# A state-space mixer's rotated scan, computed in place in the PSUM accumulators

## The chip, the cores and the metric

The kernel runs on one core of one Trainium2 chip. The metric is the device time of one execution, in microseconds (us).

## The reference

The kernel computes a two-layer encoder trunk over 512 tokens of width 1024, all in float32. The first layer mixes tokens with a diagonal complex state space (64 groups of 16 channels, 64 complex states per group), the second with an attention; each is followed by a gated feed-forward layer with a short convolution. The change lies in the state space:

```python
def s5_mixer(xn, w_in, ...):
    u = (xn @ w_in).astype(f32)
    a_bar = jnp.exp(lam * dt)
    b_bar = ((a_bar - 1.0) / lam)[..., None] * b_mat
    bu = jnp.einsum('tbgh,gph->tbgp', u_t.astype(jnp.complex64), b_bar)
    a_cum, s = lax.associative_scan(binop, (a_elems, bu), axis=0)
    s = s + a_cum * h0[None]
    y = jnp.einsum('tbgp,ghp->tbgh', s, c_mat).real
    g = jax.nn.gelu(y + d_skip * u)
    val, gate = jnp.split(g @ w_glu, 2, axis=-1)
    return val * jax.nn.sigmoid(gate)
```

## The kernel before

The 512 tokens are cut into 64 steps of 8 tokens. Within a step a small triangular matrix gives the output directly, and a state is carried only from step to step. The 1024 channels go through in four blocks, q = 0 to 3, of 16 groups each. For one block the work is this:

- `project` multiplies the normed input with the weight (three passes of split float32 on TensorE), `turn` transposes the result.
- `weights` (L1136, its products at L821 to L823) builds on VectorE (DVE) the matrices that inject a step into the state, six operations of 128 x 512 for each half block. They write their products to scratch tiles `tt1` and `tt2`, two buffers each, all operands in SBUF. `turn_weights` transposes the matrices on TensorE.
- `rotations` builds a table `tab` of cosines and sines, on DVE for q = 0, 1 and on GpSimd (POOL) for q = 2, 3; it has one buffer.
- `inject` (L1226) accumulates a block's injected steps in two PSUM banks, 4 (real parts) and 5 (imaginary parts), `self.pv[q]`, each 128 partitions x 512 (8 pairs of groups x 64 steps). No other work of this stage uses these banks.
- `states` (L1239) turns the two banks by the table (L1253 to L1256), so that the complex recurrence becomes two real ones, and scans them (L1258) with the decay `dec`. `rotate` (L1261) turns the result back (L1268, L1269) and writes the states into the tiles `p_s`, one step later (L1272, four operations of 64 partitions x 504).
- `outs` computes output matrices `w2d` on POOL, copied by DMA into `p_w`; `lags` and `toeplitz` make the triangular matrix, by way of a tile `p_ktt` (DVE L1185).
- `output` (L1275) multiplies with that matrix (L1284) and, at L1287, the states `p_s` with `p_w`; ScalarE (ACT) applies the GELU, and `turn_output` (L1301) transposes into bank 7, the bank that `lags` uses as well.

Sixteen DVE operations make the states of a block:

```python
for o, x, y, op in ((v[0], cs, sn, ALU.add), (v[1], sn, cs, ALU.subtract)):
    t1, t2 = tmp()
    tt(out=t1, in0=pv[0], in1=x, op=ALU.mult)
    tt(out=t2, in0=pv[1], in1=y, op=ALU.mult)
```

Only these four products read PSUM; the two sums, two scans, four products and four last operations read two tensors from SBUF each.

The order of TensorE's work is written out by hand in the list `ORDER` (L750): in it `output` of a block always stands ahead of the next block's `inject`. A number in the list runs that many steps of filler on TensorE: the projections of later blocks, then the first half of the gate's matrix product. The order on DVE, ACT, POOL and the DMA queue SP is made by a scheduler when the kernel is built. Weights arrive by DMA in `t_wraw` (three buffers), ACT rounds them to `t_whi`, and the rest `t_wlo` is subtracted on DVE, in this stage mostly on POOL (L130).

Of the kernel before, what the change touches and what calls it, by code (L numbers as in the profile page):

```python
# [7 lines left out]
F32 = mybir.dt.float32  # L8
# [3 lines left out]
ALU = mybir.AluOpType  # L12
PSUM = bass.MemoryType.PSUM

P = 128
T = 512
# [702 lines left out]
C = T // L  # L719
# [58 lines left out]
def flat(t):  # L778
    n = len(t.shape) - 1
    names = "abcd"[:n]  # L780
    return t.rearrange(f"p {' '.join(names)} -> p ({' '.join(names)})")
# [64 lines left out]
class S5:  # L846
# [286 lines left out]
    def tmp(self, shape):  # L1133
        return lambda: (self.t(shape, F32, "tt1", 2), self.t(shape, F32, "tt2", 2))
# [104 lines left out]
    def states(self, q):  # L1239

        nc = self.nc
        K = [P, 8, C]
        dec = self.t(K, F32, "dec")
        nc.scalar.copy(dec, self.rmag[:, 8 * q : 8 * q + 8].unsqueeze(2).broadcast_to(K))
        nc.gpsimd.memset(dec[:, :, 0:1], 0.0)
        pv = self.pv[q]
        cs, sn = (t.rearrange("p a b c -> p (a b c)") for t in self.tab[q])
        tt = nc.vector.tensor_tensor
        v = [flat(self.t(K, F32, f"v{k}")) for k in range(2)]
        tmp = self.tmp([P, T])  # L1250
        for o, x, y, op in ((v[0], cs, sn, ALU.add), (v[1], sn, cs, ALU.subtract)):
            t1, t2 = tmp()
            tt(out=t1, in0=pv[0], in1=x, op=ALU.mult)  # L1253
            tt(out=t2, in0=pv[1], in1=y, op=ALU.mult)
            a, b = (t1, t2) if op == ALU.add else (t2, t1)
            tt(out=o, in0=a, in1=b, op=op)  # L1256
        for k in range(2):
            nc.vector.tensor_tensor_scan(v[k], flat(dec), v[k], 0.0, ALU.mult, ALU.add)  # L1258
        self.rotate(q, [t.rearrange("p (a b) -> p a b", a=8) for t in v], self.tab[q])

    def rotate(self, q, st, tab):  # L1261
        nc = self.nc
        w = lambda t: t[:, :, 0 : C - 1]
        cs, sn = (w(t.rearrange("p a b c -> p a (b c)")) for t in tab)
        tmp = self.tmp([P, 8, C])
        for k, (x, y, op) in enumerate(((cs, sn, ALU.subtract), (sn, cs, ALU.add))):
            t1, t2 = (w(t) for t in tmp())
            nc.vector.tensor_tensor(out=t1, in0=x, in1=w(st[0]), op=ALU.mult)  # L1268
            nc.vector.tensor_tensor(out=t2, in0=y, in1=w(st[1]), op=ALU.mult)  # L1269
            for g in range(2):  # L1270
                pp = slice(64 * g, 64 * g + 64)
                nc.vector.tensor_tensor(  # L1272
                    out=self.s[q % 2][g][64 * k : 64 * k + 64, :, 1:C], in0=t1[pp], in1=t2[pp], op=op)

    def output(self, q, half):  # L1275

# [242 lines left out]
```

## Time and profile before

| What | us |
|---|---|
| median of 3 runs | 1286.46 (1284.4 to 1286.83) |
| the profiled execution, its own time | 1292.35 |
| its span, first to last instruction | 1290.6 |
| busy in the span: PE, DVE, ACT, POOL | 1227.5, 820.9, 541.8, 159.4 |
| granted TensorE clock, mean of the span | 0.972 of full speed |

The profiled execution is 5.9 us longer than the median, and 1.75 us of its time lies outside the span. Starts are in us from the span's start; PE is TensorE's matmuls, PEld its weight loads. The stage that holds the change lies from about 60 to 210 us.

### The profile page before, as it was taken

The page shows a single profiled execution, that of the slowest core. Times are in us where ns is not written, and L with a number is a line of the kernel's source. Part 1 is how long each engine was busy: PE and PEld are TensorE (multiplying, and loading weights), DVE is VectorE, ACT ScalarE, POOL GpSimd, SP SyncE. Part 2 cuts the span into 40 slices and gives each one's busy share as a digit, 9 for nine tenths or more (in the row PEclk, how much of TensorE's full clock was granted, in tenths as well). Part 3 has the DMA queues.
Part 4 walks back from the last instruction along what each step waited for, and adds up shares of the span by engine and source line. Part 5 has one row for each costly group of instructions (what it writes and reads, how often), then busy time and mean ns, then how long its engine had stood idle before and what let it go on. Part 6 is the DMA issues. An engine that isn't in the chain of part 4 may idle for free. (4 is left out here: it accounts for less than half of the span.)

```text
span 1290.6 us, 17189 instructions
## 1 busy us (share of the span) xinstructions
PE 1227.5 (95%) x6815; PEld 1020.9 (79%) x6815; DVE 820.9 (64%) x1252; ACT 541.8 (42%) x869; POOL 159.4 (12%) x133
## 2 busy tenths in 40 slices
PE   7666779999999999999999999999999999999998
PEld 7566667788888888888899888877688888888887
DVE  8997874587655555333368988987675555553222
ACT  7434433344433333222347666654443343332110
POOL 5848662000000000000000000000300000000000
PEclk9778889999999999999999999999999999999999
DMA  7222232323333333333322212112133333332230
GB/s 191 74 74 65 53 93 74 96 84 98 98 98 98 98 98 94 91 90 100 101 83 65 72 61 66 50 49 60 39 115 96 87 96 98 98 98 98 97 129 35
DMA packets 162379, 111.68 MB, mean 87 GB/s; under 512 B 7452, under 2 KB 151868, under 8 KB 162236
## 3 DMA queue, kind: packets, MB, share of 16 engines
q1 hardware_dynamic: 161724, 109.55, 28.9%
q8 instruction: 53, 0.87, 0.3%
q10 hardware_dynamic: 576, 1.05, 0.2%
q14 instruction: 26, 0.21, 0.1%
HBM read 101.93 MB, written 2.10 MB: 81 GB/s over the span
## 5 line engine op out<-in xcount | busy, mean ns | idle before, releaser
L249 PE MATMUL b<-t_xhi,t_whi 128*128 128x512 f32 x864 | 337.2, 393 | 1.4 <-ACT p_w L1327 1.4
L250 PE MATMUL b<-t_xlo,t_whi 128*128 128x512 f32 x864 | 337.4, 391 | 0.8 <-DVE t_xlo L168 0.7
L251 PE MATMUL b<-t_xhi,t_wlo 128*128 128x512 f32 x864 | 337.5, 391 | 0.2 <-DVE t_wlo L130 0.2
L116 ACT CAST t_whi<-t_wraw 128x1024 fp32r<-128x1024 f32 (+1 forms) x166 | 172.5, 1041 | 357.9 <-PE b L250 243.9
L130 DVE TENSOR_TENSOR t_wlo<-t_wraw,t_whi 128x1024 fp32r<-128x1024 f32 x152 | 184.8, 1217 | 155.7 <-ACT t_whi L116 155.0
L249 PEld LDWEIGHTS b<-t_xhi,t_whi 128*128 128x128 f32 x864 | 162.7, 188 | 37.8 <-issue 2.1
L250 PEld LDWEIGHTS b<-t_xlo,t_whi 128*128 128x128 f32 x864 | 162.6, 188 | 36.6 <-DVE t_xlo L168 2.6
L251 PEld LDWEIGHTS b<-t_xhi,t_wlo 128*128 128x128 f32 x864 | 162.5, 188 | 34.7 <-DVE t_wlo L130 0.6
L457 PE MATMUL b<-t_whi,t_xhi 128*128 128x256 f32 x384 | 109.6, 286 | 0.0
L458 PE MATMUL b<-t_wlo,t_xhi 128*128 128x256 f32 x384 | 109.2, 285 | 0.0
L459 PE MATMUL b<-t_whi,t_xlo 128*128 128x256 f32 x384 | 108.7, 285 | 0.0
L314 DVE TENSOR_TENSOR p_fg<-b,p_rsrow 128x512 f32<-128x512 f32 x44 | 30.4, 690 | 87.0 <-PE b L251 80.6
L325 DVE TENSOR_TENSOR p_fv<-b,p_rsrow 128x512 f32<-128x512 f32 x44 | 30.3, 689 | 69.6 <-PE b L251 69.6
L457 PEld LDWEIGHTS b<-t_whi,t_xhi 128*128 128x128 f32 x384 | 73.3, 191 | 1.6 <-issue 1.2
L459 PEld LDWEIGHTS b<-t_whi,t_xlo 128*128 128x128 f32 x384 | 73.1, 191 | 1.5 <-issue 1.4
L458 PEld LDWEIGHTS b<-t_wlo,t_xhi 128*128 128x128 f32 x384 | 73.4, 191 | 0.3
L249 PE MATMUL b<-p_ahi,t_whi 128*128 128x512 f32 x176 | 69.3, 394 | 0.0
L250 PE MATMUL b<-p_alo,t_whi 128*128 128x512 f32 x176 | 69.3, 394 | 0.0
L251 PE MATMUL b<-p_ahi,t_wlo 128*128 128x512 f32 x176 | 69.3, 394 | 0.0
L348 PE MATMUL b<-t_wlo,p_ahi 128*128 128x512 f32 x176 | 69.3, 394 | 0.0
L347 PE MATMUL b<-t_whi,p_ahi 128*128 128x512 f32 x176 | 69.0, 392 | 0.0
L349 PE MATMUL b<-t_whi,p_alo 128*128 128x512 f32 x176 | 68.3, 388 | 0.0
(304 smaller groups left out, 1989.6 us busy)
## 6 DMA issues: line engine op xcount, KB each, us to landing
t_wraw<-in_ffn_w_up_dram SPq DMA_DIRECT2D x88, 512.0 KB, 3.9
t_wraw<-in_ffn_w_down_dram SPq DMA_DIRECT2D x30, 512.0 KB, 3.4
t_wraw<-in_a_w_glu_dram SPq DMA_DIRECT2D x16, 512.0 KB, 3.6
t_wraw<-in_w_kv_dram SPq DMA_DIRECT2D x16, 512.0 KB, 3.4
t_wraw<-in_ffn_w_down_dram SPq DMA_DIRECT2D x16, 448.0 KB, 3.6
t_wraw<-in_a_w_in_dram SPq DMA_DIRECT2D x8, 512.0 KB, 3.7
p_w<-p_w2d SPq DMA_DIRECT2D x32, 128.0 KB, 2.3
t_wraw<-in_b_w_q_dram SPq DMA_DIRECT2D x8, 512.0 KB, 4.2
```

Source lines behind the costliest of these rows:

```text
L116: nc.scalar.copy(hi, t)
L130: eng.tensor_tensor(out=lo, in0=t, in1=hi, op=ALU.subtract)
L249: nc.tensor.matmul(ps, whi, xhi, start=start, stop=False)
L250: nc.tensor.matmul(ps, whi, xlo, start=False, stop=False)
L251: nc.tensor.matmul(ps, wlo, xhi, start=False, stop=stop)
L314: nc.vector.tensor_tensor(out=g, in0=pg, in1=rr, op=ALU.mult)
L347: nc.tensor.matmul(pss[tb], xh, whi[:, j], start=k + j == 0, stop=False)
L348: nc.tensor.matmul(pss[tb], xh, wlo[:, j], start=False, stop=False)
L349: nc.tensor.matmul(pss[tb], xl, whi[:, j], start=False, stop=st)
L457: nc.tensor.matmul(reg[tb], xh, whi[:, j], start=st, stop=False, skip_group_check=True)
L458: nc.tensor.matmul(reg[tb], xh, wlo[:, j], start=False, stop=False, skip_group_check=True)
L459: nc.tensor.matmul(reg[tb], xl, whi[:, j], start=False, stop=k == 7, skip_group_check=True)
```

## The change

The two banks are rotated, scanned and rotated back where they are. A block's states are still sixteen DVE operations of the same sizes, two of them scans. The scratch tiles `v0` and `v1` are gone, only the two products with the sine go to `tt1` and `tt2`, each time they are needed, and every one of the sixteen has one operand in PSUM and one in SBUF; eight of them write PSUM (four products with the cosine, two sums, two scans), the others SBUF. On the way back the products take all 64 steps instead of 63. `rotate` is merged into `states`, and the lines behind move up by seven.

```diff
--- before.py
+++ after.py
@@ -1243,34 +1243,27 @@
         dec = self.t(K, F32, "dec")
         nc.scalar.copy(dec, self.rmag[:, 8 * q : 8 * q + 8].unsqueeze(2).broadcast_to(K))
         nc.gpsimd.memset(dec[:, :, 0:1], 0.0)
-        pv = self.pv[q]
+        pv = [t[:, :] for t in self.pv[q]]
         cs, sn = (t.rearrange("p a b c -> p (a b c)") for t in self.tab[q])
         tt = nc.vector.tensor_tensor
-        v = [flat(self.t(K, F32, f"v{k}")) for k in range(2)]
-        tmp = self.tmp([P, T])
-        for o, x, y, op in ((v[0], cs, sn, ALU.add), (v[1], sn, cs, ALU.subtract)):
-            t1, t2 = tmp()
-            tt(out=t1, in0=pv[0], in1=x, op=ALU.mult)
-            tt(out=t2, in0=pv[1], in1=y, op=ALU.mult)
-            a, b = (t1, t2) if op == ALU.add else (t2, t1)
-            tt(out=o, in0=a, in1=b, op=op)
-        for k in range(2):
-            nc.vector.tensor_tensor_scan(v[k], flat(dec), v[k], 0.0, ALU.mult, ALU.add)
-        self.rotate(q, [t.rearrange("p (a b) -> p a b", a=8) for t in v], self.tab[q])
-
-    def rotate(self, q, st, tab):
-        nc = self.nc
-        w = lambda t: t[:, :, 0 : C - 1]
-        cs, sn = (w(t.rearrange("p a b c -> p a (b c)")) for t in tab)
-        tmp = self.tmp([P, 8, C])
-        for k, (x, y, op) in enumerate(((cs, sn, ALU.subtract), (sn, cs, ALU.add))):
-            t1, t2 = (w(t) for t in tmp())
-            nc.vector.tensor_tensor(out=t1, in0=x, in1=w(st[0]), op=ALU.mult)
-            nc.vector.tensor_tensor(out=t2, in0=y, in1=w(st[1]), op=ALU.mult)
+
+        t1, t2 = self.tmp([P, T])()
+        tt(out=t1, in0=pv[1], in1=sn, op=ALU.mult)
+        tt(out=t2, in0=pv[0], in1=sn, op=ALU.mult)
+        for k, (t, op) in enumerate(((t1, ALU.add), (t2, ALU.subtract))):
+            tt(out=pv[k], in0=pv[k], in1=cs, op=ALU.mult)
+            tt(out=pv[k], in0=pv[k], in1=t, op=op)
+            nc.vector.tensor_tensor_scan(pv[k], flat(dec), pv[k], 0.0, ALU.mult, ALU.add)
+
+        w = lambda t: t.rearrange("p (a b) -> p a b", a=8)[:, :, 0 : C - 1]
+        t1, t2 = self.tmp([P, T])()
+        tt(out=t1, in0=pv[1], in1=sn, op=ALU.mult)
+        tt(out=t2, in0=pv[0], in1=sn, op=ALU.mult)
+        for k, (t, op) in enumerate(((t1, ALU.subtract), (t2, ALU.add))):
+            tt(out=pv[k], in0=pv[k], in1=cs, op=ALU.mult)
             for g in range(2):
                 pp = slice(64 * g, 64 * g + 64)
-                nc.vector.tensor_tensor(
-                    out=self.s[q % 2][g][64 * k : 64 * k + 64, :, 1:C], in0=t1[pp], in1=t2[pp], op=op)
+                tt(out=self.s[q % 2][g][64 * k : 64 * k + 64, :, 1:C], in0=w(pv[k])[pp], in1=w(t)[pp], op=op)
 
     def output(self, q, half):
```

The scheduler moves some instructions, since scratch buffers come free at other times.

DVE, the second half of the states of block 0 (`b_4_850` and `b_5_851` are the two banks, `p_tt_…` the scratch). Before:

```order
L1258 SCALAR_TENSOR_TENSOR p_v_899<-p_dec,p_v_899 128x512
L1258 SCALAR_TENSOR_TENSOR p_v_900<-p_dec,p_v_900 128x512
L1268 TENSOR_TENSOR p_tt_913<-p_tab_868,p_v_899 128x8x63
L1268 TENSOR_TENSOR p_tt_919<-p_tab_869,p_v_899 128x8x63
L1269 TENSOR_TENSOR p_tt_914<-p_tab_869,p_v_900 128x8x63
L1269 TENSOR_TENSOR p_tt_920<-p_tab_868,p_v_900 128x8x63
L1272 TENSOR_TENSOR p_s_144<-p_tt_913,p_tt_914 64x8x63
L1272 TENSOR_TENSOR p_s_145<-p_tt_913,p_tt_914 64x8x63
L1272 TENSOR_TENSOR p_s_144<-p_tt_919,p_tt_920 64x8x63
L1272 TENSOR_TENSOR p_s_145<-p_tt_919,p_tt_920 64x8x63
```

Now:

```order
L1256 SCALAR_TENSOR_TENSOR b_4_850<-p_dec,b_4_850 128x512
L1256 SCALAR_TENSOR_TENSOR b_5_851<-p_dec,b_5_851 128x512
L1261 TENSOR_TENSOR p_tt_910<-b_4_850,p_tab_869 128x512
L1263 TENSOR_TENSOR b_4_850<-b_4_850,p_tab_868 128x512
L822 TENSOR_TENSOR p_tt_1088<-p_gim,p_b_430 128x512
L1260 TENSOR_TENSOR p_tt_909<-b_5_851,p_tab_869 128x512
L1263 TENSOR_TENSOR b_5_851<-b_5_851,p_tab_868 128x512
L821 TENSOR_TENSOR p_tt_1087<-p_gre,p_b_429 128x512
L1266 TENSOR_TENSOR p_s_144<-b_4_850,p_tt_909 64x8x63
L1266 TENSOR_TENSOR p_s_145<-b_4_850,p_tt_909 64x8x63
L1266 TENSOR_TENSOR p_s_144<-b_5_851,p_tt_910 64x8x63
L1266 TENSOR_TENSOR p_s_145<-b_5_851,p_tt_910 64x8x63
```

Two products of the next block's weights (L822, L821), which had stood behind the states, now stand within them, ahead of the operations that write `p_s`. The same holds for blocks 1 and 2; in block 3 nothing is drawn in.

DVE, from the last `p_s` of block 2 to the `p_ktt` behind it. Before:

```order
L1272 TENSOR_TENSOR p_s_144<-p_tt_1836,p_tt_1837 64x8x63
L1272 TENSOR_TENSOR p_s_145<-p_tt_1836,p_tt_1837 64x8x63
L821 TENSOR_TENSOR p_tt_1885<-p_gre,p_b_429 128x512
L822 TENSOR_TENSOR p_tt_1886<-p_gim,p_b_430 128x512
L821 TENSOR_TENSOR p_tt_1890<-p_gre,p_b_430 128x512
L822 TENSOR_TENSOR p_tt_1891<-p_gim,p_b_429 128x512
L823 TENSOR_TENSOR p_w_1883<-p_tt_1885,p_tt_1886 128x512
L823 TENSOR_TENSOR p_w_1884<-p_tt_1890,p_tt_1891 128x512
L1185 SCALAR_TENSOR_TENSOR p_ktt<-p_eye,p_gain,b_7_1941 128x16
```

Now:

```order
L1266 TENSOR_TENSOR p_s_145<-b_5_1666,p_tt_1815 64x8x63
L823 TENSOR_TENSOR p_w_1865<-p_tt_1867,p_tt_1868 128x512
L821 TENSOR_TENSOR p_tt_1872<-p_gre,p_b_430 128x512
L822 TENSOR_TENSOR p_tt_1873<-p_gim,p_b_429 128x512
L823 TENSOR_TENSOR p_w_1866<-p_tt_1872,p_tt_1873 128x512
L1185 SCALAR_TENSOR_TENSOR p_ktt<-p_eye,p_gain,b_7_1923 128x16
```

Four operations of the weights stand between them where there were six.

POOL, the rotation table of block 2 (`p_tab`) and the splits of streamed weights (`t_wlo`) around it. Before:

```order
L130 TENSOR_TENSOR t_wlo<-t_wraw,t_whi 128x1024
L821 TENSOR_TENSOR p_tp_1789<-p_e16c 128x512
L822 TENSOR_TENSOR p_tp_1790<-p_e16s 128x512
L1245 MEMSET p_dec 128x8
L130 TENSOR_TENSOR t_wlo<-t_wraw,t_whi 128x1024
L823 TENSOR_TENSOR p_tab_1787<-p_tp_1789,p_tp_1790 128x512
```

Now:

```order
L821 TENSOR_TENSOR p_tp_1777<-p_e16c 128x512
L822 TENSOR_TENSOR p_tp_1778<-p_e16s 128x512
L130 TENSOR_TENSOR t_wlo<-t_wraw,t_whi 128x1024
L1245 MEMSET p_dec 128x8
L823 TENSOR_TENSOR p_tab_1775<-p_tp_1777,p_tp_1778 128x512
L130 TENSOR_TENSOR t_wlo<-t_wraw,t_whi 128x1024
```

The splits have moved behind two products and behind the first half of the table. SP issues two of the streamed weight loads one place earlier, ahead of copies of `p_w` and `p_tz`. TensorE and ACT keep their order.

## Rows read from the trace of the kernel before

**Rows 1.** The page's busy time of TensorE: us, share of the span, instructions.

```profile
PE 1227.5 (95%) x6815; PEld 1020.9 (79%) x6815; DVE 820.9 (64%) x1252; ACT 541.8 (42%) x869; POOL 159.4 (12%) x133
```

**Rows 2.** Windows: stretch, us, busy us (instructions) PE PEld DVE ACT POOL, PEclk, DMA, GB/s.

```profile
90.00:95.00 5.00, 4.02 (x29) 3.30 (x29) 4.94 (x8) 0.05 (x1) 1.06 (x1) 0.50 0.00 0
...
127.00:132.00 5.00, 4.22 (x36) 3.53 (x34) 4.97 (x4) 0.52 (x1) 4.84 (x4) 0.54 0.00 0
...
150.00:156.00 6.00, 6.00 (x77) 5.04 (x79) 1.01 (x3) 2.35 (x7) 5.41 (x5) 0.50 0.03 8
...
230.00:1290.00 1060.00, 1053.96 (x5329) 871.01 (x5327) 637.12 (x997) 437.10 (x658) 23.96 (x24) 1.00 0.29 86
```

**Rows 3.** Waits of PE, 60 to 230 us: waiter, releaser, us in total, times, longest.

```profile
PE b L1287 <- DVE p_s L1272: 21.9, 8, 8.3
PE b L1301 <- DVE p_ktt L1185: 11.0, 2, 6.0
```

**Rows 4.** Timeline of DVE, the states of block 0: start us, us, line, tiles.

```profile
70.87 1.29 DVE L1253 TENSOR_TENSOR p_tt<-b,p_tab 128x512 f32<-128x512 f32 x2 [1.21 <-PE b L1235]
...
74.47 4.49 DVE L1258 TENSOR_TENSOR_SCAN p_v<-p_dec,p_v 128x512 f32<-128x512 f32 x2
...
85.37 6.24 DVE L1272 TENSOR_TENSOR p_s<-p_tt,p_tt 64x504 f32<-64x504 f32 x4
```

**Rows 5.** Timeline of DVE, the states of blocks 1 to 3 and the `p_ktt` behind.

```profile
108.51 1.28 DVE L1253 TENSOR_TENSOR p_tt<-b,p_tab 128x512 f32<-128x512 f32 x2
...
122.82 5.26 DVE L1272 TENSOR_TENSOR p_s<-p_tt,p_tt 64x504 f32<-64x504 f32 x4
...
149.70 0.22 DVE L1185 SCALAR_TENSOR_TENSOR p_ktt<-p_eye,p_gain,b 128x16 f32<-128x16 f32 x1
...
156.57 1.29 DVE L1253 TENSOR_TENSOR p_tt<-b,p_tab 128x512 f32<-128x512 f32 x2 [1.15 <-POOL p_tp L821]
...
160.18 1.22 DVE L1258 TENSOR_TENSOR_SCAN p_v<-p_dec,p_v 128x512 f32<-128x512 f32 x1
...
164.92 6.59 DVE L1272 TENSOR_TENSOR p_s<-p_tt,p_tt 64x504 f32<-64x504 f32 x4
...
180.74 0.22 DVE L1185 SCALAR_TENSOR_TENSOR p_ktt<-p_eye,p_gain,b 128x16 f32<-128x16 f32 x1
...
188.24 1.29 DVE L1253 TENSOR_TENSOR p_tt<-b,p_tab 128x512 f32<-128x512 f32 x2 [4.77 <-PE b L1235]
...
200.50 4.91 DVE L1272 TENSOR_TENSOR p_s<-p_tt,p_tt 64x504 f32<-64x504 f32 x4
```

**Rows 6.** DVE's L1272: its group (us, mean ns), then its durations, min/median/max.

```profile
L1272 DVE TENSOR_TENSOR p_s<-p_tt,p_tt 64x504 f32<-64x504 f32 x16 | 22.7, 1419 | 0.3
...
L1272 DVE TENSOR_TENSOR p_s<-p_tt,p_tt x16: 665/1454/2817, 85.4 to 202.6; 64x504 f32<-64x504 f32 x16
```

**Rows 7.** Timeline of POOL: one shape, beside SBUF-only DVE work, then beside L1253.

```profile
84.87 1.54 POOL L1210 TENSOR_TENSOR p_tp<-p_pwim,p_c 128x512 f32<-128x512 f32 x1
...
108.39 1.11 POOL L1210 TENSOR_TENSOR p_tp<-p_pwim,p_c 128x512 f32<-128x512 f32 x1
```

**Rows 8.** Timeline of PE, matmuls that waited: start us, us, line, tiles, [idle before].

```profile
90.16 0.69 PE L1287 MATMUL b<-p_w,p_s 128*64 128x128 f32 x2 [8.26 <-DVE p_s L1272]
...
126.67 0.69 PE L1287 MATMUL b<-p_w,p_s 128*64 128x128 f32 x2 [7.45 <-DVE p_s L1272]
...
149.97 1.11 PE L1301 MATMUL b<-t_ident,p_gl 64*128 64x64 f32 x8 [4.92 <-DVE p_ktt L1185]
...
169.90 0.43 PE L1287 MATMUL b<-p_w,p_s 128*64 128x128 f32 x2 [0.29 <-DVE p_s L1272]
...
171.56 0.32 PE L1287 MATMUL b<-p_w,p_s 128*64 128x128 f32 x1 [1.23 <-DVE p_s L1272]
...
181.01 1.11 PE L1301 MATMUL b<-t_ident,p_gl 64*128 64x64 f32 x8 [6.05 <-DVE p_ktt L1185]
...
205.46 0.32 PE L1287 MATMUL b<-p_w,p_s 128*64 128x128 f32 x1 [2.42 <-DVE p_s L1272]
```

## The prediction

> **What bounds the kernel now.** First the page: TensorE is busy for 1227.5 of 1290.6 us [rows 1], so only the time in which it stands still or runs slowly can be won. The windows show that from 230 us on it is busy for 1053.96 of 1060 us at full clock [rows 2]: whatever shift the first 210 us gain or lose reaches the end unchanged. The waits of PE between 60 and 210 us name two releasers, both on DVE: `p_s`, the states, 21.9 us in eight waits, and `p_ktt`, 11.0 us in two [rows 3]. Together 33 us. `p_ktt` is a tiny operation, late only because DVE works through its queue in order, behind the states and the weights.
>
> Next, what DVE does in the states. In block 0 six operations take from 70.87 to 74.47, so 0.60 us each [rows 4]. The two scans behind them take 4.49, that is 2.25 each, and the four last operations 6.24, that is 1.56 each. In block 2 a scan takes 1.22 [rows 5], and of the last operations the quickest takes 0.665 and the mean 1.419 [rows 6]. So the same operation has two prices. What sets them is POOL: one shape of its takes 1.54 beside an SBUF-only operation of DVE and 1.11 beside the two L1253 at 108.51 [rows 7], which themselves take their usual 1.28 for two [rows 5]. Two SBUF operands on DVE and work on POOL slow each other; with one operand in PSUM neither is slowed. The states pay this in twelve of sixteen operations.
>
> **The change, part by part.** The count of operations is unchanged, so nothing is saved but this overlap; every one of the sixteen now has one PSUM operand.
>
> *Price of a block.* Fourteen operations at 0.60 make 8.4. The two scans have 1.22 as the price without POOL, less the 0.08 by which neighbours overlap (two L1253 take 1.28, 0.60 and 0.68): 2.3. Together 10.7 us. Nothing in the trace writes PSUM from DVE, and no scan reads it. Below, nothing is left to gain beyond 0.60 and 1.14; above, the ends are 1.56 for an operation and 2.25 for a scan, which POOL's overlap costs now. I take the low prices, since the nearest row, an operation of the same size that reads PSUM, has them with POOL at work. A scan that stays at 2.25 would add 2.2 us a block.
>
> *What is drawn in.* In blocks 0 to 2 two products of the weights now stand ahead of `p_s`. They are SBUF-only: 0.60 to 1.56 each. In blocks 0 and 1 POOL is at work, so I take 1.56, 3.1 for two; in block 2 POOL is idle for most of the time, so 1.2. Blocks 0 and 1 then take 13.8, block 2 11.9. Block 3 draws nothing in, but has, as before, two small operations of others within it, 0.8: 11.5. Now they take 20.7, 19.6, 14.9 and 17.2 (70.87 to 91.61, 108.51 to 128.08, 156.57 to 171.51, 188.24 to 205.41) [rows 4, 5].
>
> *What of it reaches TensorE,* in order, each step starting from the shift of the one before:
>
> 1. Block 0 ends at 70.87 + 13.8 = 84.7 instead of 91.6: 6.9 us. TensorE got to its wait at 90.16 - 8.26 = 81.9 [rows 8], so it still waits and takes over all of the 6.9.
> 2. From there to the states of block 1 the chain runs over TensorE and ACT and moves as a whole. Start 101.6, end 115.4 instead of 128.1: shift 12.7. TensorE gets there at 119.2 - 6.9 = 112.3, so it waits again.
> 3. From 128.08 to the `p_ktt` at 149.70 DVE does nineteen operations, 1.14 each with the overlap as it is. Two of them were drawn in; seventeen take 19.3, so 134.7: shift 15.0. TensorE would be there at 145.05 - 12.7 = 132.3 and waits 2.4.
> 4. Block 2 starts at 141.6 and ends at 153.5. TensorE gets there at 169.61 - 15.0 = 154.6. Both waits, 0.29 and 1.23 [rows 8], are gone: shift 16.5.
> 5. To the `p_ktt` at 180.74 six operations take 9.2 now, 1.54 each. Four remain, 6.2: 159.7, a shift of 21.0. TensorE is there at 174.96 - 16.5 = 158.5.
> 6. Block 3 starts at 167.2 and ends at 178.7; TensorE wants the last of it at 203.0 - 21.0 = 182.0, and its wait of 2.42 is gone: shift 23.4.
>
> *What is moved elsewhere.* On POOL the weight splits stand one to two products later, 1.1 to 1.5 each [rows 7]; no wait of TensorE on a split stands beside the long ones of the stage [rows 3], and POOL's own products get shorter. I cost it at nothing; uncovered it would be some 3 us once. The loads that SP issues earlier pass copies of `p_w` and `p_tz` whose readers TensorE starts only after the states: nothing, as long as the buffer for the load is free. The banks are held until the last `p_s`, but TensorE's hand-written order has `output` of the block, which waits for that, ahead of the next `inject`: no new wait.
>
> The sum is -23.4. The profiled execution would come to 1292.35 - 23.4 = 1269.0. It lies 5.9 us above the median of the runs shown; from the median, 1286.46 - 23.4 = **1263 us**.
>
> [...] The rows give 0.60 us for an operation with a PSUM operand and for one without [rows 4], so PSUM itself costs nothing here. [...]
>
> **The rivals.**
>
> *A. The overlap comes back on the weights.* POOL's work is the same; what no longer meets the states may meet the weights' products. For it: the last six, with POOL at work, already take 1.54 each. Against it: POOL's own operations get shorter, so it is done sooner. If step 3's sixteen products all take 1.56, that is 25.6 with the split, `p_ktt` comes at 141.0 and the shift there is 8.7. Block 2 with 13.8 then ends at 161.7, shift 9.8 at its `p_s` and, with four products at 1.56, 12.8 at the next `p_ktt`. With the last 2.4 that is 15: 1271 us.
>
> [...]
>
> *C. Writing PSUM is dear.* Eight operations a block write to PSUM from DVE, two of them scans, and read the same bank. If each took 1.2 us more (three times 0.60 for a plain one), a block would take 9.6 more: 23.4, 23.4, 21.5 and 21.1. Block 0 is then 2.7 late, block 1 another 3.8; the two drawn-in products give back 2.3 in front of `p_ktt`; block 2 loses 6.6 and gets 3.1 back, block 3 loses 3.9. That is 11.6 slower: 1298 us. It turns from a gain to a loss at about 0.8 us more for each. Against it is only that reading costs nothing.
>
> *D. Nothing changes.* TensorE could be held at the same points by something else than the states, a `p_w` copy or a split. No such releaser stands beside the two [rows 3].
>
> **How the numbers follow.** The forecast, 1257 to 1269, has a chance of 0.55; A 0.20, B 0.15, C 0.06, D 0.04. The range leaves out C and D and half of what A and B could overshoot. Its upper end is A with both scans of blocks 0 and 1 at 2.25 (4.4 us): 1275. Its lower end is B with the drawn-in products of blocks 0 and 1 at 0.60 (1.9 us): 1253. A measurement of this kernel can tell about 0.2%, 2.6 us. Forecast, A and B are all faster by more than that; C is slower and D within: 0.90, 0.04 and 0.06.
>
> **What would show it.** The products, sums and last operations of the states at 0.60 to 0.68 us, the scans at about 1.2, with POOL at work beside them; a block's states in 11 to 14 us from first to last; TensorE's total wait for `p_s` below 8 us and for `p_ktt` below 6; POOL's operations beside the states at 1.1. The forecast is wrong if a PSUM-writing operation takes clearly more than 0.7, if the weights' products behind the states go to 1.56 throughout (A), or if a new releaser, a split or a `p_w` copy, stands ahead of TensorE's waits.

## The result and the profile after

| What | before | after |
|---|---|---|
| median of 4 runs, us | 1286.3 (1284.4 to 1286.83) | 1267.6 (1265.56 to 1269.87) |
| the profiled execution, us | 1292.35 | 1265.56 |
| its span, us | 1290.6 | 1263.8 |
| granted TensorE clock, mean of the span | 0.972 | 0.983 |

The ratio is 0.9858, with an interval of 0.9838 to 0.9877: faster by 18.7 us, where 23.4 were forecast. The two profiled executions lie 26.8 us apart; why more than the medians is told with the steps. The page's busy line after, to set against [rows 1]:

```profile
PE 1221.5 (97%) x6815; PEld 1016.3 (80%) x6815; DVE 802.1 (63%) x1252; ACT 542.3 (43%) x869; POOL 152.8 (12%) x133
```

The counts are the same. DVE is 18.8 us less busy and POOL 6.6, with not one instruction fewer: operations on both engines have become shorter. By line, from 60 to 215 us (DVE; busy us, mean ns, then idle before):

```profile
L822 DVE TENSOR_TENSOR p_tt<-p_gim,p_b 128x512 f32<-128x512 f32 x12 | 18.7, 1562 | 0.0
...
L1266 DVE TENSOR_TENSOR p_s<-b,p_tt 64x504 f32<-64x504 f32 x16 | 10.8, 678 | 0.3
L1256 DVE TENSOR_TENSOR_SCAN b<-p_dec,b 128x512 f32<-128x512 f32 x8 | 9.5, 1214 | 0.0
L1254 DVE TENSOR_TENSOR b<-b,p_tab 128x512 f32<-128x512 f32 x8 | 5.5, 690 | 0.0
```

L1266 is L1272 of before: 678 ns where it was 1419 [rows 6]. The scans (L1256) take 1.21 us each throughout, and an operation that reads and writes its own bank (L1254) takes 0.69. The weights' products, all SBUF, are now the long ones: L822 has a mean of 1.56. The waits of PE from 60 to 230 us, against [rows 3] (L1280 was L1287, L1294 was L1301):

```profile
PE b L1280 <- DVE p_s L1266: 6.0, 5, 2.3
PE b L1192 <- DVE p_ktt L1185: 5.3, 2, 4.2
PE b L1179 <- DVE t_xlo L165: 4.6, 1, 4.6
...
PE b L1294 <- DVE p_ktt L1185: 1.4, 2, 1.1
```

The wait for `p_s` has gone from 21.9 to 6.0 and that of L1294 for `p_ktt` from 11.0 to 1.4. The second row, another `p_ktt`, was there before with 5.3. The third is new in this size: a split of activations, `t_xlo`, in DVE's queue behind the weights' products. DVE's timeline after, which answers to [rows 4, 5]:

```profile
71.26 0.69 DVE L1252 TENSOR_TENSOR p_tt<-b,p_tab 128x512 f32<-128x512 f32 x1 [1.61 <-PE b L1235]
...
74.86 2.33 DVE L1256 TENSOR_TENSOR_SCAN b<-p_dec,b 128x512 f32<-128x512 f32 x2
...
78.28 1.46 DVE L822 TENSOR_TENSOR p_tt<-p_gim,p_b 128x512 f32<-128x512 f32 x1
...
80.86 1.68 DVE L821 TENSOR_TENSOR p_tt<-p_gre,p_b 128x512 f32<-128x512 f32 x1
82.45 2.79 DVE L1266 TENSOR_TENSOR p_s<-b,p_tt 64x504 f32<-64x504 f32 x4
...
111.76 2.79 DVE L1266 TENSOR_TENSOR p_s<-b,p_tt 64x504 f32<-64x504 f32 x4
114.58 1.24 DVE L823 TENSOR_TENSOR p_w<-p_tt,p_tt 128x512 f32<-128x512 f32 x1
...
117.21 1.55 DVE L822 TENSOR_TENSOR p_tt<-p_gim,p_b 128x512 f32<-128x512 f32 x1
...
137.21 0.22 DVE L1185 SCALAR_TENSOR_TENSOR p_ktt<-p_eye,p_gain,b 128x16 f32<-128x16 f32 x1
...
141.46 0.69 DVE L1252 TENSOR_TENSOR p_tt<-b,p_tab 128x512 f32<-128x512 f32 x1 [0.32 <-issue]
...
148.61 2.44 DVE L822 TENSOR_TENSOR p_tt<-p_gim,p_b 128x512 f32<-128x512 f32 x1
...
152.78 2.79 DVE L1266 TENSOR_TENSOR p_s<-b,p_tt 64x504 f32<-64x504 f32 x4
...
161.43 0.23 DVE L1185 SCALAR_TENSOR_TENSOR p_ktt<-p_eye,p_gain,b 128x16 f32<-128x16 f32 x1
...
166.62 0.69 DVE L1252 TENSOR_TENSOR p_tt<-b,p_tab 128x512 f32<-128x512 f32 x1 [2.86 <-PE b L1235]
...
175.59 2.79 DVE L1266 TENSOR_TENSOR p_s<-b,p_tt 64x504 f32<-64x504 f32 x4
```

Two scans took 4.49 in block 0 and now 2.33; four last operations took 6.24, 5.26, 6.59 and 4.91, and now 2.79 in every block. Within the blocks only operations of others that were drawn in are still slowed beside POOL: 1.46, 1.68 and 2.44 us (78.28, 80.86, 148.61), and one of 1.32 at 108.72. The two others take 0.68 (111.16, 152.18). POOL's side after, against [rows 7]:

```profile
102.48 1.12 POOL L1210 TENSOR_TENSOR p_tp<-p_pwim,p_c 128x512 f32<-128x512 f32 x1
...
121.38 1.55 POOL L1210 TENSOR_TENSOR p_tp<-p_pwim,p_c 128x512 f32<-128x512 f32 x1
...
148.10 2.41 POOL L130 TENSOR_TENSOR t_wlo<-t_wraw,t_whi 128x1024 fp32r<-128x1024 f32 x1 [3.86 <-ACT t_whi L116]
```

Beside the states of block 1 the shape takes 1.12, beside the weights' products at 121 us 1.55. The `t_wlo` at 148.10 is what makes the drawn-in L822 at 148.61 take 2.44. Windows after, columns as in [rows 2] (the third number from the end is the granted clock):

```profile
90.00:95.00 5.00, 5.00 (x62) 4.62 (x60) 5.00 (x6) 3.56 (x7) 3.26 (x3) 1.00 0.49 108
...
118.00:124.00 6.00, 6.00 (x50) 5.64 (x49) 6.00 (x6) 1.57 (x3) 4.77 (x4) 0.65 0.60 139
...
136.00:142.00 6.00, 5.71 (x105) 4.57 (x104) 2.98 (x6) 4.75 (x12) 5.79 (x4) 1.00 0.03 10
...
180.00:186.00 6.00, 6.00 (x63) 4.94 (x64) 0.00 (x0) 3.59 (x6) 2.38 (x1) 1.00 0.49 145
```

Behind the wait for the states of block 0 the clock is 1.00 where it was 0.50 [rows 2]; behind that of block 1 it is still low for a while (0.65); behind `p_ktt` it is 1.00.

### The profile page after: what moved, and what is told of

The parts are those of the page before. It is cut to its first block, busy times and chain, and to the rows that moved or that the text cites. A ratio compares the mean times of both kernels' runs of the same rounds, so it can differ in the third digit from the quotient of the medians.

```text
span 1263.8 us, 17184 instructions
## 1 busy us (share of the span) xinstructions
PE 1221.5 (97%) x6815; PEld 1016.3 (80%) x6815; DVE 802.1 (63%) x1252; ACT 542.3 (43%) x869; POOL 152.8 (12%) x133
```

## The experiments

All ratios are to the kernel before, run beside it on the same chip.

**1. The kernel before, again.**

> The kernel before, unchanged. The profiled execution that the prediction was made from took 1292.35 us, 6 us more than the median. If that was the one execution's chance, the shifts that its rows give are sound and only the median's distance is off: this run's profiled execution takes 1284 to 1288 and one of its stretches is about 6 us shorter, outside the states. If profiling adds 6 us to this kernel, it takes 1290 to 1294 again. The states of block 0 take 20 to 21 us, of blocks 1 to 3 19 to 20, 14 to 16 and 16 to 18 either way.

Edit: none. Measured 1285.4 us (ratio 1.0001, 0.9981 to 1.0021). Of its ten executions seven lie between 1284.99 and 1285.63, three between 1291.86 and 1292.93; 21 others of the same kernel, timed beside it, fill the gap from 1284.81 up to 1292.47. So the profiled execution of before, 1292.35, stands at the long end and the one profiled here, 1285.16, at the short end: profiling does not add the 6 us. Of the blocks' lengths expected here two were missed: the states of blocks 0 to 3 take 20.8, 20.1, 18.6 and 14.4, so they change from one execution to the next. PE's timeline here:

```profile
147.11 0.70 PE L1301 MATMUL b<-t_ident,p_gl 64*128 64x64 f32 x8 [2.41 <-DVE p_ktt L1185]
...
209.93 0.71 PE L1301 MATMUL b<-t_ident,p_gl 64*128 64x64 f32 x8
```

The wait for the first `p_ktt` is 2.41 instead of 4.92 [rows 8]: the operations between the states of block 1 and that `p_ktt` take 19.5 us instead of 21.6, presumably because they happen to meet POOL less. The eight transposes behind it take 0.70 instead of 1.11, and the granted clock is 1.00 in 147 to 153 where it was 0.50 in 150 to 156. From that `p_ktt` to the states of block 2 it takes 4.24 us instead of 6.87. At the start of block 2 this execution is 5.5 us ahead, and by L1301's last group 7.24 (209.93 against 217.17), the whole difference of the two.

**2. The changed kernel, twice again.**

> The changed kernel, unchanged, on the same chip. Ratio 0.984 to 0.988. States of block 0 in 14.0 us, blocks 1 and 2 in 12.9 to 14.1, block 3 in 11.8.

> The changed kernel again, beside the one before it, for their difference on one chip: 1264 to 1270.

Edit: none. 1268.63 us (ratio 0.9857, 0.9832 to 0.9882), and with the last experiment 1267.12 (0.983, 0.9806 to 0.9854). In the profile of the first, `p_ktt` behind block 1 comes at 138.05, and block 0 takes 14.1 us. TensorE's rows there, then two windows:

```profile
133.59 1.08 PE L1179 MATMUL b<-p_w,p_cm 128*32 128x128 f32 x16 [6.43 <-DVE t_xlo L165]
...
139.99 0.71 PE L1294 MATMUL b<-t_ident,p_gl 64*128 64x64 f32 x8
```

```profile
130.00:136.00 6.00, 2.41 (x23) 1.99 (x24) 5.97 (x6) 1.47 (x6) 5.84 (x5) 0.50 0.20 44
136.00:142.00 6.00, 6.00 (x67) 5.11 (x69) 2.27 (x4) 4.22 (x8) 2.26 (x2) 0.71 0.02 4
```

The wait for `t_xlo` is 6.4, the longest single one; the granted clock in 130 to 136 is 0.50 (0.72 in the first profile), and 0.71 in the next 6 us (1.00). TensorE comes to the transposes at 139.99, when `p_ktt` is long there, and from `p_ktt` to the states of block 2 it takes 5.9 us, where the first profile of the change has 4.25. The other repeat shows the same: 6.4 for `t_xlo`, clock 0.50 and 0.77 in these windows, 5.9 us. So of three profiles of the change one has the short stretch.

**3. The same order, with the states in SBUF.**

> The order of the operations as in the changed kernel (two sine products to scratch, everything else in place), but in place in two SBUF tiles; only the first four products read PSUM. Theory, overlap with POOL: twelve operations have two SBUF operands again, so the states take 17 to 22 us in blocks 0 and 1 (with three products of the weights drawn in), and the time is that of the kernel before within 5 us: 1281 to 1291. Rival, the saving comes from the fewer scratch tiles and from the new order on DVE: 1265 to 1272.

```diff
+        v = [flat(self.t(K, F32, f"v{k}")) for k in range(2)]
...
-            tt(out=pv[k], in0=pv[k], in1=cs, op=ALU.mult)
-            tt(out=pv[k], in0=pv[k], in1=t, op=op)
-            nc.vector.tensor_tensor_scan(pv[k], flat(dec), pv[k], 0.0, ALU.mult, ALU.add)
+            tt(out=v[k], in0=pv[k], in1=cs, op=ALU.mult)
+            tt(out=v[k], in0=v[k], in1=t, op=op)
+            nc.vector.tensor_tensor_scan(v[k], flat(dec), v[k], 0.0, ALU.mult, ALU.add)
+        pv = v
```

1285.22 us (0.9975, 0.996 to 0.999): nearly all of the gain is gone. DVE by line, from 60 to 215 us:

```profile
L1268 DVE TENSOR_TENSOR p_s<-p_v,p_tt 64x504 f32<-64x504 f32 x16 | 21.1, 1321 | 0.3
...
L1257 DVE TENSOR_TENSOR_SCAN p_v<-p_dec,p_v 128x512 f32<-128x512 f32 x8 | 14.7, 1857 | 0.0
```

The mean of a last operation is back at 1.32 and of a scan at 1.86; PE's wait for `p_s` is 27.3. So it is not the new order of the sixteen operations that pays, but the operand in PSUM. Three products of the weights are drawn in here, and blocks 0 and 1 take 22.9 and 20.6 us. The two scratch tiles are back too; that it is not their absence that pays shows in experiment 6, whose second half has them and still gains 13.8.

**4. The states unbroken.** The states and the weights keep the order of the program on DVE, so that nothing is drawn into a block's states.

> The changed kernel, with the operations of the states and of the weights held in program order on DVE, so that no product of the weights stands within the states, and the small operations behind the states of block 1 come ahead of the weights that are not needed yet. Theory, DVE's queue in front of p_s and p_ktt is what TensorE still waits for: states of blocks 0 and 1 in 11 us, waits for p_s under 3 us in total, p_ktt behind block 1 some 5 us earlier, 1257 to 1264. Rival, the products have to be done anyway and only change places: 1265 to 1270.

```diff
-        tt = nc.vector.tensor_tensor
+        tt = lambda **k: self.e.tc.keep_in_program_order(nc.vector.tensor_tensor(**k))
...
-        cmul(self.nc.vector, self.tmp(W), w1[0], w1[1], gb, bb)
+        cmul(Kept(self.e), self.tmp(W), w1[0], w1[1], gb, bb)
```

(`Kept` does for the weights what the first lambda does; the scans are kept likewise, and the four products stand ahead of the two sums.) 1277.42 us (0.9938, 0.9914 to 0.9962), some 9 us slower than the change, outside both expectations; its runs spread from 1273.45 to 1282.70, and the profile is of the shortest. The states do shorten as both said: block 0 takes 11.0 us (69.25 to 80.26), as the prediction priced it. But the wait for `p_s`, expected below 3, is 8.4, and PE's waits from 60 to 230 us show a new one:

```profile
PE b L1163 <- DVE p_w L851: 10.7, 2, 7.1
PE b L1291 <- DVE p_s L1256: 8.4, 7, 3.6
PE b L1305 <- DVE p_ktt L1193: 6.2, 1, 6.2
```

What was put off is the weights, and TensorE needs those as well. DVE's timeline here shows the rest:

```profile
122.89 1.78 DVE L851 TENSOR_TENSOR p_tt<-p_gre,p_b 128x512 f32<-128x512 f32 x1
...
141.69 0.21 DVE L1193 SCALAR_TENSOR_TENSOR p_ktt<-p_eye,p_gain,b 128x16 f32<-128x16 f32 x1
...
144.84 0.23 DVE L1464 COPY t_vc<-b 128x66 f32<-128x66 f32 x1 [2.94 <-PE b L1463]
```

Twelve operations of the weights stand between 122.89 and 140.91, nine of them at 1.44 to 1.78, ahead of the `p_ktt` that comes at 141.69, later than in the change and not earlier as expected; and a small copy, `t_vc`, that waits for TensorE now stands ahead of the states of block 2. They start at 144.99 (141.46 in the change). The two drawn-in products cost a block's states 2 to 3 us, but putting them off lost more, as the sum shows. How the 9 us divide between the weights, `t_vc` and the other order of products and sums was not taken apart.

**5. Before and after with a quieter POOL.**

> The kernel before, with the 48 products and sums that POOL makes for the output matrices left out (ACT copies the coefficients instead, two copies for each half block, so the outputs are not the reference's). POOL keeps the weight splits and the tables of blocks 2 and 3. Theory, overlap with POOL: the SBUF-only operations of the states fall towards 0.6 to 0.7 us, scans to 1.2 where no split or table runs; blocks 0, 1 and 3 in 11 to 16 us; 1262 to 1278. Rival, the SBUF-only operations are slow by themselves or by their order: blocks 0 and 1 in 19 to 21 us, 1280 to 1290.

> The changed kernel with the same work of POOL left out. Theory, overlap with POOL: the change now gains only what splits and tables cost, 2 to 9 us against the quiet kernel before (18.7 with POOL at work), and the weights' products behind the states fall to 0.6 to 0.8 us as well: 1254 to 1264. Rival: the same gain of 15 to 20 us between the two quiet kernels.

```diff
-        mul(tp[0], ar, cr)
-        mul(tp[1], ai, cn)
-        nc.gpsimd.tensor_tensor(out=w2d[0], in0=tp[0], in1=tp[1], op=ALU.add)
...
+        for k in range(2):
+            nc.scalar.copy(w2d[k], self.c[k][:, sl].unsqueeze(2).broadcast_to(W))
```

Before: 1258.31 us (0.978, 0.9766 to 0.9795), faster than either theory expected; after: 1249.03 (0.971, 0.9696 to 0.9725), faster than expected too. The difference between the two forms is 9.3 us instead of 18.7, just above the 2 to 9 expected. Where POOL is idle, the form of before has the low prices too: its last operations of block 0 take 2.78 for four, while those of block 1 stand beside what POOL still does:

```profile
75.31 2.78 DVE L1263 TENSOR_TENSOR p_s<-p_tt,p_tt 64x504 f32<-64x504 f32 x4
...
105.73 5.26 DVE L1263 TENSOR_TENSOR p_s<-p_tt,p_tt 64x504 f32<-64x504 f32 x4
```

So the partner of the overlap is POOL. The weights' products stay near 1.0 in the mean, where 0.6 to 0.8 was expected, as the tables and splits still meet them (1.55 each at 105 to 110 us), and both kernels have a new wait of TensorE of some 5 us for `p_u`, an operation of ACT, which now makes the copies. The tables and the splits stayed on POOL, so the remaining 9.3 us are not a bound on a gain without it; taking those away as well was not tried.

**6. Each half of the change alone.** First the way in (products, sums) in PSUM, with a scan that writes SBUF and the way back in SBUF; then the way in in SBUF, with a scan that writes the bank and the way back in PSUM.

> The changed kernel, in place in PSUM only up to the scans, which write SBUF tiles; the rotation back has two SBUF operands again. Theory, overlap with POOL: the scans of blocks 0 and 1 go from 2.25 to 1.14, the sums to 0.60, some 5 us in all four blocks, and three products of the weights drawn in ahead of p_s take part of it back: 1279 to 1287. Rival, the scan is what matters: 1268 to 1274.

```diff
-            nc.vector.tensor_tensor_scan(pv[k], flat(dec), pv[k], 0.0, ALU.mult, ALU.add)
+            nc.vector.tensor_tensor_scan(v[k], flat(dec), pv[k], 0.0, ALU.mult, ALU.add)
+        pv = v
```

> The changed kernel, with the first rotation in SBUF tiles; the scan reads SBUF and writes the PSUM banks, and the rotation back is in place there. Theory, overlap with POOL: most of the gain is in the eight operations behind the scan (23 of 29 us of DVE time in the rows of before); scans with two SBUF operands stay near 2.25 beside POOL: 1269 to 1276. Rival, the scan is what matters: 1280 to 1287.

```diff
-            tt(out=pv[k], in0=pv[k], in1=cs, op=ALU.mult)
-            tt(out=pv[k], in0=pv[k], in1=t, op=op)
-            nc.vector.tensor_tensor_scan(pv[k], flat(dec), pv[k], 0.0, ALU.mult, ALU.add)
+            tt(out=v[k], in0=pv[k], in1=cs, op=ALU.mult)
+            tt(out=v[k], in0=v[k], in1=t, op=op)
+            nc.vector.tensor_tensor_scan(pv[k], flat(dec), v[k], 0.0, ALU.mult, ALU.add)
```

The way in alone: 1278.26 us (0.9937, 0.9922 to 0.9952), 8.0 faster than before, a little more than expected. The way back alone: 1272.45 (0.9893, 0.9876 to 0.9909), 13.8 faster. Together 21.8, a little more than the 18.7 of both; presumably they shorten the same waits, which was not followed up. By line on DVE, from 60 to 215 us, the way in alone:

```profile
L1268 DVE TENSOR_TENSOR p_s<-p_v,p_tt 64x504 f32<-64x504 f32 x16 | 21.2, 1327 | 0.3
...
L1257 DVE TENSOR_TENSOR_SCAN p_v<-p_dec,b 128x512 f32<-128x512 f32 x8 | 9.5, 1204 | 0.0
```

The same view of the way back alone:

```profile
L1257 DVE TENSOR_TENSOR_SCAN b<-p_dec,p_v 128x512 f32<-128x512 f32 x8 | 11.7, 1484 | 0.0
L1267 DVE TENSOR_TENSOR p_s<-b,p_tt 64x504 f32<-64x504 f32 x16 | 10.8, 678 | 0.3
```

An operation that reads a bank has the low price throughout (by line, means of 678 to 690 ns, and 1204 for a scan); one that reads SBUF only has it where POOL leaves it alone (2.78 for four in experiment 5). The scan shows it best: reading a bank and writing SBUF it takes 1.20; reading SBUF and writing a bank it takes 1.48 in the mean, 2.34 for the two of block 0 and 4.49, the full price of the overlap, for the two of block 1.

**7. One of the weights' scratch products in a bank.** The two banks are free until a block's inject, so from the second half of block 1 on the first product of a pair goes there, and the sum reads it there.

> The changed kernel, with one of the two scratch products of the weights written to the PSUM banks 4 and 5, from the second half of block 1 on, while the banks wait for the next block; the ten sums L823 then have one PSUM operand. The products still read two SBUF tensors. Theory, the weights in front of p_ktt are slowed by POOL: the sums fall from 1.5 to 0.6 us, the p_ktt behind block 1 comes 3 to 5 us earlier, 1259 to 1265. Rival, POOL's operations only meet the products instead, or a bank is now waited for by inject: 1266 to 1272, with a new wait of TensorE's L1235 on DVE in the second case.

```diff
-        cmul(self.nc.vector, self.tmp(W), w1[0], w1[1], gb, bb)
+        tmp = self.tmp(W)
+        if (q, half) > (1, 0):
+            ps = iter((4, 5))
+            tmp = lambda: (
+                self.e.bank(next(ps)).rearrange("p (a l h) -> p a l h", a=4, l=L), self.t(W, F32, "tt2", 2))
+        cmul(self.nc.vector, tmp, w1[0], w1[1], gb, bb)
```

1263.54 us in five runs (1261.72 to 1264.87; 0.9805, 0.9781 to 0.9829), beside 1267.12 (1266.71 to 1267.78) of the change: 3.6 us better, and the fastest version here that leaves no work out. The two ratio intervals overlap, since the kernel before scatters; the runs beside each other don't, though one of experiment 2 (1264.37) lies among them. DVE by line, from 60 to 215 us:

```profile
L821 DVE TENSOR_TENSOR b<-p_gre,p_b 128x512 f32<-128x512 f32 x10 | 13.5, 1368 | 0.1
...
L823 DVE TENSOR_TENSOR p_w<-b,p_tt 128x512 f32<-128x512 f32 x10 | 6.4, 682 | 0.1
```

The sums fall from a mean of 1200 to 682 ns. The products into the bank stay at 1368, since both their inputs lie in SBUF. `p_ktt` comes at 133.52, where the profile of the change taken beside it has 137.36, and the wait for `t_xlo` is 3.3 instead of 6.4. The inject has a new wait of 2.1 for a sum, as the second theory said; that it gives part of the gain back is likely, not shown.

## Why the prediction was right, and where it missed

**The cause** was right. The same sixteen operations in the same order with SBUF operands lose the gain (experiment 3), and each half alone gains where its operations read a bank (experiment 6). The runs add the price of the overlap for an operation with two SBUF inputs: 0.60 to some 1.56 us on DVE, and 1.11 to 1.55 on POOL.

**What would show it** came as said: `p_s` 6.0 (below 8), `p_ktt` at L1294 1.4 (below 6), POOL beside the states at 1.1. **The price of a block** was right. Without anything drawn in, experiment 4 gives 11.0 us for 10.7. The low ends were the right ones: 0.68 to 0.69 for an operation, overlap with its neighbour included, and 2.33 for two scans, with POOL at work.

**The steps**, as time lost (+) or won (-) against the forecast, in the profiled execution:

| Step | predicted | measured | against the forecast |
|---|---|---|---|
| 1. block 0 ends | 84.7 | 85.24 | +0.5 |
| 2. block 1 starts, ends | 101.6, 115.4 | 101.60, 114.55 | -0.5, -0.9 |
| 3. the `p_ktt` | 134.7 | 137.21 | +3.4 |
| 4. block 2 starts, ends | 141.6, 153.5 | 141.46, 155.57 | -2.6, +2.2 |
| 5. the `p_ktt` | 159.7 | 161.43 | -0.3 |
| 6. block 3 starts | 167.2 | 166.62 | -2.3 |

- *Step 3 was mis-sized.* "1.14 each with the overlap as it is" did not hold: the seventeen operations took 22.6 us (114.58 to 137.21), 1.33 each. POOL was at work from 115 to 138 but for 1.5 us, and the long products met it. This is rival A in part: 3.4 of the 6.3 us that it set. Experiment 7 takes some of these overlaps away and has `p_ktt` earlier by 3.7. The path also lacked a wait: TensorE was forecast at the `p_ktt` at 132.3, but came there at 137.2, after 4.6 us of wait for `t_xlo`, where it was 1.7 before. The sum has no term for it; in the two other profiles of the change this wait is 6.4, and it ends last, not `p_ktt`.
- *In step 4 a drawn-in product was under-priced:* 1.2 for two, on the ground that POOL is idle for most of block 2. It was not at 148 us; the two took 3.1. So the waits at the end of block 2, forecast as gone, stayed with 1.9 us where they had been 1.5.
- *The granted clock, the B of the chances, gave back nearly as much.* From the first `p_ktt` to the states of block 2 it took 4.25 us instead of 6.87, from the second to block 3 5.19 instead of 7.50, and 0.5 in step 2. The stretch behind the first of them was at 0.50 before [rows 2] and is at 1.00 in 136 to 142 now. TensorE's rows after show it (compare [rows 8]):

```profile
137.49 0.71 PE L1294 MATMUL b<-t_ident,p_gl 64*128 64x64 f32 x8 [0.29 <-DVE p_ktt L1185]
...
161.71 0.71 PE L1294 MATMUL b<-t_ident,p_gl 64*128 64x64 f32 x8 [1.15 <-DVE p_ktt L1185]
...
168.61 0.71 PE L1294 MATMUL b<-t_ident,p_gl 64*128 64x64 f32 x8
...
190.26 0.71 PE L1294 MATMUL b<-t_ident,p_gl 64*128 64x64 f32 x8
```

Behind waits of 0.29 and 1.15 the same eight transposes take 0.71, behind 4.92 and 6.05 they took 1.11. But for the first `p_ktt` this is one profile of three: in the two others the stretch takes 5.9 us, so the clock gives back 1.0 there and not 2.6 (experiment 2). The execution of before profiled in experiment 1 has the short stretch too, 4.24. For step 6, two pairs of transposes and a wait in the kernel before:

```profile
190.23 0.70 PE L1301 MATMUL b<-t_ident,p_gl 64*128 64x64 f32 x8
...
202.62 0.43 PE L1287 MATMUL b<-p_w,p_s 128*64 128x128 f32 x2 [0.69 <-DVE p_s L1272]
...
217.17 0.71 PE L1301 MATMUL b<-t_ident,p_gl 64*128 64x64 f32 x8
```

- *Step 6 named one wait of two.* The shift is 21.6 at the first pair (190.23 and 168.61) and 26.9 at the last (217.17 and 190.26). In between lie 2.42 [rows 8] and 0.69 us of wait for `p_s`, of which the prediction counted the first. That leaves 2.2; the clock of 0.89 and 0.82 in 202 to 208 and 208 to 214 before, against 1.00 after, accounts for 1.7 of it, and 0.5 stay open.

So in the profiled executions the products cost 4.9 us more than forecast (the first five steps without the clock), the clock gave back up to 7.6 (0.5, 2.6, 2.3, 2.2) and the second wait 0.7: 26.8 instead of 23.4. Neither A nor B was the likeliest case; both happened in part, and that they almost cancelled is luck. The lower end of the range, 1253, has 8 us of clock in it; no run shows that term, what the runs showed is the up to 7.6 here, and 1.0 in place of 2.6 behind the first `p_ktt` in the two other profiles of the change.

**From the profile to the median.** The prediction subtracted from the median a shift worked out on an execution 6 us above it. That was its other error, and the one that decides the number: part of the 23.4 are waits, and the low clock behind them, that the shorter executions of before don't have (experiment 1: 2.41 for 4.92, and a clock of 1.00 behind it, where it was 0.50). Between that execution and the changed one 19.6 us remain (1285.16 and 1265.56), and the profiled execution after lies 2.0 below its median: the one of experiment 2, with the longer stretch behind `p_ktt`, is 2.5 us longer (1268.08). So 26.8 less 6.05 less 2.04 is 18.7. The forecast of 1263 is 4.6 too low because these 8.1 us outweigh the 3.4 by which the shift was forecast too small; the result lies in the forecast's own band and in the range, in part because these errors run against each other.

**The price of a bank.** No price of its own for an operation that reads PSUM is seen: 0.68 to 0.69 with a bank read, 0.68 without one and without POOL (after, 67.02 and 68.23). Taking the states into SBUF with the first products, as experiment 3 does, gives 1285.22 us, 16.6 slower than the change run beside it (1268.63).

**The other rivals.** C, writing PSUM dear: 0.69 for a written bank; it fell. D, nothing changes: a new releaser did appear, `t_xlo`, a split, as D said one might, but with 4.6 us (6.4 in the two other profiles, the longest single wait) instead of all. Pricing the splits at nothing was wrong in that, and this one of the prediction's own signs of being wrong came in part.

## What to carry to other kernels

Look up what the same operation costs in two places of one trace: 0.68 and 1.59 us for a weights' product of one shape (after, 124.00 and 126.28), the longer one with POOL at work beside it throughout, is a larger lever than its count. Where VectorE and GpSimd work at once, an operand that is already in PSUM was best left there, in this kernel, for as long as its bank was free (1268.63 us against 1285.22 in experiment 3). And profile the kernels, before and after, more than once: a sum made on one execution carries with it what is that execution's own, here 6 us before and 2 after.

## What the runs showed of the hardware that was not expected

- It is the inputs that decide, not the output. A product of two SBUF inputs into a bank still takes 1.37 in the mean (experiment 7), a scan of SBUF inputs into a bank 4.49 for two (experiment 6).
- Executions of one program spread from 1284.8 to 1292.9 us with nothing changed (experiment 1). The two that were profiled differ in how long TensorE waits for one tiny operation on DVE, and in the clock behind that wait: 5.5 of the 7.2 us are there by the start of block 2.
- Taking 48 products off POOL made the kernel before 28 us faster, though no wait of TensorE in [rows 3] names POOL. That is more than the change itself gains. The outputs of these kernels lack the work, and ACT makes copies in its place; how much of the gain comes from the weights' products was not taken apart.
